# An encoder layer in one stream of matrix work: final blocks moved ahead of gate columns, output products by weight unit, last attention tiles split in place

## The chip, the cores and the metric

The kernel runs on one core of a Trainium2 chip. The metric is the device time in microseconds (us). One execution was profiled; its span is the time from its first to its last instruction. TensorE (PE) does the matrix products, PEld is its loading of weights, VectorE (DVE) and ScalarE (ACT) do elementwise work, GpSimd (POOL) little here, and SyncE (SP) issues nearly all DMAs.

## The reference

One layer of a bidirectional encoder, for two sequences: a short one of 1024 tokens (s = 0) and a long one of 2048 (s = 1), each with the same 16 meta tokens in front; the model width is 1024.

```python
xn = rmsnorm(h, g_pre)
proj = xn @ w_in + b_in                        # 1024 -> 6672 columns
na_q, na_k, na_v, na_z, ml_qk, ml_v, ml_z, ml_o, ml_g, mg = split(proj)
ya = (neighbourhood_attention(na_q, na_k, na_v, na_rpb) * silu(na_z)) @ w_a
yb = (mlstm_branch(ml_qk, ml_v, ml_g, ml_o, conv_w, head_g) * silu(ml_z)) @ w_b
ga, gb = split(sigmoid(mg))
y = (ga * ya + gb * yb) @ w_out
return h + rmsnorm(y, g_post)                  # meta tokens dropped
```

The attention looks at a window of 8 rows by 16 columns of a grid 64 wide, plus the meta tokens. The mLSTM runs forwards and backwards over the sequence; its queries and keys pass a convolution of three taps first. All is float32.

## The kernel before

**Precision.** Each operand of a dense product is split into a high part (a rounding to a shorter float32 form, made by ScalarE) and a low part (the rest, made by VectorE); each product is three matmuls: high x high, high x low, low x high (`mm3`, lines 170 to 172; `tm_unit`, lines 619 to 621; `prods`, lines 1875 to 1877). Weights are handled in units of 512 KB. At first use a unit is loaded raw (`wraw`), split (`whi`, `wlo`, lines 258 to 270) and both parts are written to DRAM; later uses load the two parts. Four units are held at a time (`NBW`), and `wtake`, `wdone`, `wpump` hand them out, give them back and fetch the next.

**Two streams.** `dense` yields the dense products in the order of `PLAN`, each step with its cost in us (0.235 for a matmul of 512 columns, 0.12 for 256). `sparse` yields the steps of the branches in the order of `STEPS`: mLSTM 0, attention 0, mLSTM 1, attention 1, each step with a cost. `run` puts the two together: after each sparse step it takes dense work worth the step's cost times the entry's rate (the last number in `STEPS`; a few "fix" steps are taken at 1). TensorE executes in exactly this order. The other engines' order is made by a planner with a cost model, except for instructions given to `behind`, which keep the program's order. A sparse stage starts only when what it needs is in `done`; until then `run` takes dense work alone. `beside` is called at each dense step: it steps the convolutions (`pstep`, `cprep`) and the background generators (`bg`).

**Dense work.** An entry (s, t0, letters) of `PLAN` is a group over 1024 tokens: column tiles of 128 (`fm_half`; a and k, q, z, G, h stand for mLSTM queries and keys, attention keys, queries, gates z, and the merge gates) and token-major columns (t: values, output gates; `tm_unit`). `layout` orders the jobs of a group: some jobs of column tiles, then all of t, then the rest. "S" is a Strassen-like pass over the short sequence (`sstream`). An entry ("f", s, b) is a final block over 512 tokens (`final`): eight pairs of half merges (attention half, mLSTM half; 12 matmuls of 512 columns each) give the gated sum `mh`, `mlo`; then the output product, four quarters of 256 columns (cq) by four tiles of 128 tokens (tt), 24 matmuls of 256 columns each; then the norm with `g_post` and the residual (`final_out`). The last final block has no successor (`nxt` is None).

**What meets around the change.** The attention writes its gated output `yg` to DRAM (`YA`); `yload` loads it into `yl`, ScalarE copies the high part to `yh`, VectorE subtracts, and the merge that needs it waits for that. The output product of a token tile ends with a square on ScalarE (line 1905, with an accumulated sum) and a product with the gain on VectorE (line 1906), both from PSUM. PSUM has eight banks, three of them under the tag `pj`. The inputs of the next group are built by `build_half`: tokens are loaded, squared and summed (`rsum`), a diagonal of the factors is made (`rdiag`), spread over the partitions by a matmul (`rrows`, line 326), and the transposed tokens are scaled by it and split. Final block 0 of a sequence can start once its mLSTM is through and the attention of its rows is done.

Of the kernel before, what the change touches and what calls it, by code (L numbers as in the profile page):

```python
# [43 lines left out]
PLAN = ((0, 0, "akt"),) + FIRST + ((1, 0, "at"), (1, 1024, "akqzt"), (1, 0, "kqzGh"), (1, 1024, "Gh"), ("f", 0, 0), ("f", 0, 1), ("f", 1, 0), ("f", 1, 1), ("f", 1, 2), ("f", 1, 3))  # L44
STEPS = (("ml", 0, (), 0.78), ("na", 0, (0, 1), 1.05), ("ml", 1, (), 0.78), ("na", 1, (0, 1, 2, 3), 0.765))
# [80 lines left out]
class K:  # L126
# [3 lines left out]
    def __init__(self, tc, ins, outs):  # L130
        self.tc, self.nc = tc, tc.nc
        self.xs = []
        self.i, self.o = ins, outs
        self.wreq, self.wraw, self.wrdy, self.wout = deque(), deque(), deque(), 0
        self.wseen, self.wkept, self.xkept = set(), {}, {}
        self.rwait = {}
        self.xput, self.turn, self.last, self.turns = deque(), 0, None, False
        self.need, self.gpost = False, None
# [4 lines left out]
        self.hold, self.early = deque(), True  # L143

# [47 lines left out]
    def gain(self, name):  # L192

        g = self.wp.tile([P, D], F32, name="gain", bufs=1)
        self.nc.sync.dma_start(g, _bc(self.i[name], 0, D))
        return g
# [99 lines left out]
    def rsum(self, xs, res, first=None):  # L296
# [7 lines left out]
        for q, (xr, n) in todo:  # L304
            junk = wp.tile([P, D], mybir.dt.bfloat16, name="xsq", tag="thT", bufs=1)
            nc.scalar.activation(junk[:n], xr[:n], AF.Square, accum_out=ss[:n, q:q + 1])
            yield
# [105 lines left out]

    def build_half(self, s, t0, res):
# [370 lines left out]
    def sload(self, n, u):  # L785
# [5 lines left out]
        def get(i, j, pool, name, tag, bufs):  # L791
            x = pool.tile([P, 4 * WU], F32, name=name, tag=tag, bufs=bufs) if tag == "wraw" else pool.tile([P, 2 * 512], F32, name=name, tag=tag, bufs=bufs)
            x = x[:, :1024].rearrange("p (a c) -> p a c", a=2)
            for a in range(2):
                self.nc.sync.dma_start(x[:, a], self.i["wu"][u0 + j + 2 * a, :, 512 * i:512 * i + 512])
# [107 lines left out]
    def sstream(self, visits, nxt):  # L903
# [9 lines left out]
        for n, u in self.sorder(visits):  # L913
            s, t0, c, v = self.sdq[n]
            if u == 1:
                q = self.sq[n] = dict(done=set())
                for a in range(2):
                    q["C", a] = self.psum(("pj", "pj", "pj", "sc")[(2 * n + a) % 4], [P, 512])
                if n == 0 and len(visits) > 1 and visits[1][:2] not in self.XF:
# [48 lines left out]
    def layout(self, cols):  # L968
# [6 lines left out]
        a = max(1, min(sum(c[0] < C_GA for _, c in jobs), len(jobs) - 1))  # L975
# [21 lines left out]
    def spread(self, gen, chunks, until=None):  # L997

        steps = 22 if until is None else 12
# [246 lines left out]
    def na_out(self, np_, unit, s):  # L1246
# [15 lines left out]
        if hh and cb == 3:  # L1262
            nc.vector.tensor_tensor(yg, yg, zt, op=ALU.mult)
            nc.sync.dma_start(self.YA[s][rt][pr][:, :], yg)
# [121 lines left out]
    def cprep(self, s, h, is_k, a, b):  # L1386
# [5 lines left out]
        if s:  # L1392
            both = self.wp.tile([P, D], F32, name="cpl", tag="gain", bufs=1)[:, :804].rearrange("p (a c) -> p a c", a=2)
# [34 lines left out]
    def pstep(self):  # L1428

        while len(self.pact) < 2 - ((1, 0) in self.have) and self.pq:  # L1430
# [128 lines left out]
    def ml_outputs(self, mp, s, h, g, NB, sts, norms):  # L1559
# [23 lines left out]
        def split(b):  # L1583
            if b < NB:
                raw = raws.pop(b)
                if s and b % 3 == 2 and self.gpost is None:
# [87 lines left out]
        def finish(b):  # L1674
# [9 lines left out]
            if not a:  # L1684
                hbs[q] = mp.tile([P, 2 * CB, P], F32, name="hb", bufs=2)
# [47 lines left out]
    def ml_norm(self, mp, s, h, q, hb, tz):  # L1733
# [20 lines left out]
        for _ in range(10):  # L1754
# [8 lines left out]
    def yload(self, s, b):  # L1763
# [17 lines left out]
        late, half = [4, 5, 6, 7, 0, 1, 2, 3], None  # L1781
        while todo or late or half is not None:
# [19 lines left out]
    def final(self, s, b, nxt):  # L1802
# [21 lines left out]
        for ft, br in [(0, 1)] + [x for f in range(KT) for x in ((f + 1, 1), (f, 0)) if x[0] < KT]:  # L1824
# [3 lines left out]
            for k in range(4 * br, 4 * br + 4):  # L1828
                self.need = True
                while k not in self.yk:  # L1830
                    if next(self.ygen) == "wait" and k not in self.yk:
# [25 lines left out]
        if self.fresh:  # L1857
            self.fresh = False
            nc.vector.tensor_scalar(self.gpost, self.gpost, -0.125, None, op0=ALU.mult)
# [10 lines left out]
        def prods(p, tt, ws, k0, k1):  # L1870
            o = p[:, :256]
            xs = slice(tt * P, tt * P + P)
            for k in range(k0, k1):
                wh, wl = ws[k // 4][0][:, k % 4, :], ws[k // 4][1][:, k % 4, :]
                nc.tensor.matmul(o, mh[:, k, xs], wh, start=k == 0, stop=False)  # L1875
                nc.tensor.matmul(o, mh[:, k, xs], wl, start=False, stop=False)  # L1876
                nc.tensor.matmul(o, ml[:, k, xs], wh, start=False, stop=k == KT - 1)  # L1877

        for cqs in (((0,), (1,), (2,), (3,)) if nxt else ((0,), (1,), (2, 3))):
            wq = [self.wtake(2) for _ in cqs]  # L1880
            first = {}
            if cqs[0] == 0:
                for tt in range(2):
                    first[tt] = self.psum("pj", [P, 512])
                    prods(first[tt], tt, wq[0], 0, 7)
                    yield 21 * C256
            turns = [(tt, x) for tt in range(4) for x in zip(cqs, wq)]
            if len(cqs) > 1:
                turns[1:3] = turns[2], turns[1]
            for tt, (cq, ws) in turns:  # L1890
                if tt in first:
                    p = first[tt]
                    prods(p, tt, ws, 7, 8)
                else:
                    p = self.psum("pj", [P, 512])
                    prods(p, tt, ws, 0, 4)
                    if tt == 3:
                        self.wdone()
                    yield 12 * C256
                    prods(p, tt, ws, 4, 8)  # L1900
                if tt == 3:
                    self.wdone()
                o = p[:, :256]
                dst = yt[tt][:, cq * 256:(cq + 1) * 256]
                nc.scalar.activation(sqj, o, AF.Square, accum_out=ssq[:, tt, cq:cq + 1])
                nc.vector.tensor_tensor(dst, o, self.gpost[:, cq * 256:(cq + 1) * 256], op=ALU.mult)
                if cq == 3 and not nxt:
                    for _ in self.final_out(s, t0, yt, ssq, tt, tt + 1):
                        pass
                if nxt and hook is None:  # L1910
                    if nxt[0] != "f":
                        nres = []
                        hook = self.build_half(*nxt[:2], nres)
                    else:
                        hook = self.ystart(*nxt[1:])
                if hook:
                    next(hook, None)
                yield (3 if tt in first else 12) * C256
# [10 lines left out]
    def final_out(self, s, t0, yt, ssq, a, b):  # L1929
# [17 lines left out]
        r = self.rsqrt8(fp, sv[:, a:b], [P, b - a])  # L1947
        yield
# [14 lines left out]
    def dense(self, ctx):  # L1963
# [11 lines left out]
        for j, item in enumerate(PLAN):  # L1975
# [6 lines left out]
            if s == "f":  # L1982
                if self.gpost is None:
                    self.gpost = self.gain("g_post")
                    self.fresh = True
# [111 lines left out]
```

## Time and profile before

| | us |
|---|---|
| median of 3 runs | 2817.07 |
| lowest, highest | 2802.38, 2821.04 |
| the profiled execution | 2810.6 |
| its span | 2808.8 |
| PE busy in the span | 2728.9 |
| DVE busy | 1729.2 |
| ACT busy | 1501.9 |

The profile's page gives busy times per engine; its other views group instructions by line and tiles, list who waited for whom, follow the chain of work that ended last, and cut the span into stages. Ends of matmuls are modelled, as they are pipelined: a busy PE need not be at its peak. A matmul of 512 columns is recorded with some 0.38 us while the next starts 0.23 us after it.

### The profile page before, as it was taken

What the parts mean: (1) busy time and instruction counts of PE and PEld (TensorE: products, weight loads), DVE (VectorE), ACT (ScalarE), POOL (GpSimd) and SP (SyncE); (2) the same over time, 40 slices, a digit from 0 to 9 for tenths busy, and PEclk for the clock granted to TensorE, in tenths of its full rate; (3) what the DMA queues carried; (4) which work ended last, traced back from release to release, by engine and by line L of the source; (5) the groups of instructions that cost most, each with busy time, mean ns of one, the idle gap of its engine ahead of it and who ended that gap; (6) DMA issues with size and microseconds to landing.
All of it is one profiled execution on the core that took longest, in us unless ns stands there. A gap on an engine that the chain in (4) does not pass through costs nothing.

```text
span 2808.8 us, 47866 instructions
## 1 busy us (share of the span) xinstructions
PE 2728.9 (97%) x16840; PEld 2427.4 (86%) x16840; DVE 1729.2 (62%) x4339; ACT 1501.9 (53%) x3348; POOL 124.4 (4%) x298
## 2 busy tenths in 40 slices
PE   8999999999999999999999999999999999999988
PEld 7899988879998778999977888888888898988978
DVE  5534664534667636566624767665667868787754
ACT  5222454433446646655534666565657676777731
POOL 0220000005000000320000000000000000000000
PEclk9999999999999999999999999999999999999989
DMA  9876753396656976756586566885599989898964
GB/s 370 327 252 216 241 181 105 104 349 203 189 171 200 328 232 203 224 178 212 189 286 208 196 208 203 275 280 172 171 314 327 292 268 302 247 323 281 275 216 174
DMA packets 354676, 666.47 MB, mean 237 GB/s; under 512 B 53796, under 2 KB 159220, under 8 KB 354436
## 3 DMA queue, kind: packets, MB, share of 16 engines
q1 hardware_dynamic: 347172, 654.37, 70.4%
q0 software_dynamic: 7264, 9.04, 1.2%
q8 instruction: 133, 2.18, 0.3%
q14 instruction: 107, 0.88, 0.1%
HBM read 446.24 MB, written 216.97 MB: 236 GB/s over the span
## 4 chain that ended last, share of the span: by engine, by line
PE 75%; DMA 14%; DVE 6%; ACT 3%; issue 1%; SPq 1%; DVEq 0%; ACTq 0%; POOLq 0%; POOL 0%
PE pj L170 11%; PE pj L171 11%; PE pj L172 11%; PE pj L619 6%; PE pj L621 6%; PE pj L620 6%; PE pj L1876 3%; PE pj L1875 3%; PE pj L1877 3%; PE sm L1254 2%; PE sm L172 2%; PE tr L1240 2%; PE sm L171 2%; PE sm L170 2%; DMA qk<-cpl 1%; DMA wlo<-wl 1%
## 5 line engine op out<-in xcount | busy, mean ns | idle before, releaser
L170 PE MATMUL pj<-xh,whi 128*128 128x512 f32 (+1 forms) x1480 | 581.7, 393 | 9.8 <-ACT st L544 7.8
L171 PE MATMUL pj<-xl,whi 128*128 128x512 f32 (+1 forms) x1480 | 567.9, 384 | 0.1
L172 PE MATMUL pj<-xh,wlo 128*128 128x512 f32 (+1 forms) x1480 | 566.6, 383 | 0.3 <-DVE wlo L270 0.3
L619 PE MATMUL pj<-whi,xh 128*128 128x256 f32 (+1 forms) x1536 | 438.8, 286 | 2.1 <-DVE stT L634 2.1
L620 PE MATMUL pj<-wlo,xh 128*128 128x256 f32 (+1 forms) x1536 | 432.5, 282 | 0.0
L621 PE MATMUL pj<-whi,xl 128*128 128x256 f32 (+1 forms) x1536 | 432.4, 282 | 0.0
L170 PEld LDWEIGHTS pj<-xh,whi 128*128 128x128 f32 x1480 | 280.2, 189 | 60.5 <-ACT st L544 8.6
L172 PEld LDWEIGHTS pj<-xh,wlo 128*128 128x128 f32 x1480 | 279.8, 189 | 58.0 <-DVE wlo L270 0.5
L171 PEld LDWEIGHTS pj<-xl,whi 128*128 128x128 f32 x1480 | 280.4, 189 | 46.5 <-issue 0.5
L619 PEld LDWEIGHTS pj<-whi,xh 128*128 128x128 f32 x1536 | 289.6, 189 | 2.7 <-DVE stT L634 2.3
L620 PEld LDWEIGHTS pj<-wlo,xh 128*128 128x128 f32 x1536 | 289.4, 188 | 0.2
L621 PEld LDWEIGHTS pj<-whi,xl 128*128 128x128 f32 x1536 | 289.3, 188 | 0.0
L1875 PE MATMUL pj<-whi,mh 128*128 128x256 f32 x768 | 222.1, 289 | 6.5 <-ACT whi L269 3.7
L1876 PE MATMUL pj<-wlo,mh 128*128 128x256 f32 x768 | 218.9, 285 | 3.8 <-DMA wlo<-wl 2.1
L1877 PE MATMUL pj<-whi,mlo 128*128 128x256 f32 x768 | 218.4, 284 | 0.0
L170 PE MATMUL pj<-yh,whi 128*128 128x512 f32 x384 | 156.6, 408 | 9.7 <-ACT yh L1793 9.7
L1875 PEld LDWEIGHTS pj<-whi,mh 128*128 128x128 f32 x768 | 147.5, 192 | 8.3 <-ACT whi L269 4.1
L171 PE MATMUL pj<-yl,whi 128*128 128x512 f32 x384 | 153.2, 399 | 1.3 <-DVE yl L1778 1.3
L172 PE MATMUL pj<-yh,wlo 128*128 128x512 f32 x384 | 152.7, 398 | 0.0
L1876 PEld LDWEIGHTS pj<-wlo,mh 128*128 128x128 f32 x768 | 147.5, 192 | 5.7 <-DMA wlo<-wl 2.6
L1877 PEld LDWEIGHTS pj<-whi,mlo 128*128 128x128 f32 x768 | 147.4, 192 | 0.0
L1243 DVE TENSOR_TENSOR pts<-tr,pts 96x384 fp32r<-96x384 f32 (+2 forms) x192 | 118.6, 618 | 46.7 <-ACT pts L1242 45.8
(378 smaller groups left out, 5643.8 us busy)
## 6 DMA issues: line engine op xcount, KB each, us to landing
whi<-wh SPq DMA_DIRECT2D x152, 512.0 KB
wlo<-wl SPq DMA_DIRECT2D x152, 512.0 KB
wraw<-wu SPq DMA_DIRECT2D x64, 512.0 KB
wh<-whi SPq DMA_DIRECT2D x64, 512.0 KB
wl<-wlo SPq DMA_DIRECT2D x64, 512.0 KB
gt<-st SPq DMA_DIRECT2D x96, 256.0 KB
tg<-gt SPq DMA_DIRECT2D x96, 256.0 KB
xt<-xt SPq DMA_DIRECT2D x32, 512.0 KB
```

The lines of the kernel that those rows point to most:

```text
L170: mm(out, ah, bh, start=start, stop=False, **more)
L171: mm(out, ah, bl, start=False, stop=False, **more)
L172: mm(out, al, bh, start=False, stop=stop, **more)
L619: nc.tensor.matmul(o, xh, wh, start=k == 0, stop=False)
L620: nc.tensor.matmul(o, xh, wl, start=False, stop=False)
L621: nc.tensor.matmul(o, xl, wh, start=False, stop=k == KT - 1)
L1240: nc.tensor.transpose(pt[:ks, ch, :], pr_[:, ch * ks:(ch + 1) * ks], self.ident)
L1243: nc.vector.tensor_tensor(pts[:ks, :nb, 1, :], pt[:ks, :nb], pts[:ks, :nb, 0, :].bitcast(F32), op=ALU.subtract)
L1254: nc.tensor.matmul(av[:, cb % 2], vt[:ks, kc // 8 + ch].rearrange("p a b -> p (a b)"), pts[:ks, ch].rearrange("p a b -> p (a b)"), start=c ...
L1875: nc.tensor.matmul(o, mh[:, k, xs], wh, start=k == 0, stop=False)
L1876: nc.tensor.matmul(o, mh[:, k, xs], wl, start=False, stop=False)
L1877: nc.tensor.matmul(o, ml[:, k, xs], wh, start=False, stop=k == KT - 1)
```

## The change

1. `PLAN`: the final blocks of the short sequence stand ahead of the last group of gate columns of the long one. The rates of `STEPS` for mLSTM 1 and attention 1 become 0.81.
2. `final`: the output product goes by weight unit (half of the contraction, 512 rows, of one quarter): one unit is used for all four token tiles, whose accumulators lie two to a bank in two banks, then the second unit. In the last block this holds for two quarters; the other two go by tile as before, in another order, with four units held. In the last block two half merges change places.
3. `na_out`: when the final block that is being loaded is the one whose attention tile has just ended, `yg` is split straight into `yh`, `yl`, without DRAM.
4. `rahead`: the factors of the long sequence's first two halves are made during the Strassen pass and kept.
5. The convolutions of the long sequence use other buffers (four under the tag `xr`, which token loads use too, in place of one), two are active at a time, and `beside` steps them twice.
6. `layout`: t comes after at most two jobs of column tiles. That changes the group (1, 1024, "akqzt") alone.
7. `g_post` is loaded by quarters for each final block, and its factor of -0.125 is applied in `final_out`. `hb` has three buffers, a norm waits 12 steps in place of 10, and `build_half` is stepped faster by `spread`.

```diff
-PLAN = (... (1, 0, "kqzGh"), (1, 1024, "Gh"), ("f", 0, 0), ("f", 0, 1), ("f", 1, 0), ("f", 1, 1), ("f", 1, 2), ("f", 1, 3))
-STEPS = (("ml", 0, (), 0.78), ("na", 0, (0, 1), 1.05), ("ml", 1, (), 0.78), ("na", 1, (0, 1, 2, 3), 0.765))
+PLAN = (... (1, 0, "kqzGh"), ("f", 0, 0), ("f", 0, 1), (1, 1024, "Gh"), ("f", 1, 0), ("f", 1, 1), ("f", 1, 2), ("f", 1, 3))
+STEPS = (("ml", 0, (), 0.78), ("na", 0, (0, 1), 1.05), ("ml", 1, (), 0.81), ("na", 1, (0, 1, 2, 3), 0.81))
...
+    def gain(self, c):
+        g = self.wp.tile([P, WU], F32, name="gp", tag="bb", bufs=2)
+        self.nc.sync.dma_start(g[:, :256], _bc(self.i["g_post"], 256 * c, 256))
+        return g[:, :256]
...
+    def rahead(self, s, t0s):
+        dg = self.wp.tile([P, 2, 512], F32, name="dgs", tag="gain", bufs=1)
+        for c, t0 in enumerate(t0s):
+            toks, r = self.tokens(s, t0, range(4), self.wp, 4), []
+            for _ in range(3):
+                yield
+            yield from self.rsum(toks, r, pin=True)
+            self.rpre[s, t0] = self.rdiag(r[0], dg[:, c])
+            yield
...
         else:
-            toks, r = self.tokens(s, t0, range(4), wp, 4), []
-            yield
-            yield from self.rsum(toks, r)
-            dg = self.rdiag(r[0], toks[3][0])
+            dg = self.rpre.pop((s, t0), None)
+            if dg is None:
+                ...
...
         self.pstep()
+        if (1, 0) in self.have:
+            self.pstep()
...
-        a = max(1, min(sum(c[0] < C_GA for _, c in jobs), len(jobs) - 1))
+        a = max(1, min(2, len(jobs) - 1))
...
-            nc.sync.dma_start(self.YA[s][rt][pr][:, :], yg)
+            if self.y and self.y[0] == (s, rt) and pr in self.ylate:
+                _, yh, yl = self.y
+                nc.scalar.activation(yh[:, pr], yg, AF.Copy)
+                nc.vector.tensor_tensor(yl[:, pr], yg, yh[:, pr].bitcast(F32), op=ALU.subtract)
+                self.ylate.remove(pr)
+                self.yk.add(pr)
+            else:
+                nc.sync.dma_start(self.YA[s][rt][pr][:, :], yg)
...
-            both = self.wp.tile([P, D], F32, name="cpl", tag="gain", bufs=1)...
+            both = self.wp.tile([P, D], F32, name="cpl", tag="xr", bufs=4)...
...
-        while len(self.pact) < 2 - ((1, 0) in self.have) and self.pq:
+        while len(self.pact) < 2 and self.pq:
...
+        order = [(0, 1)] + [x for f in range(KT) for x in ((f + 1, 1), (f, 0)) if x[0] < KT]
+        if not nxt:
+            order[2:4] = order[3], order[2]
...
+        def prods(o, tt, w, a, fresh):
+            xs = slice(tt * P, tt * P + P)
+            for k in range(4):
+                f, q = 4 * a + k, w[0][:, k, :]
+                nc.tensor.matmul(o, mh[:, f, xs], q, start=fresh and f == 0, stop=False, skip_group_check=True)
+                nc.tensor.matmul(o, mh[:, f, xs], w[1][:, k, :], start=False, stop=False, skip_group_check=True)
+                nc.tensor.matmul(o, ml[:, f, xs], q, start=False, stop=f == KT - 1, skip_group_check=True)
+
+        def leave(o, tt, cq, gp):
+            nc.scalar.activation(sqj, o, AF.Square, accum_out=ssq[:, tt, cq:cq + 1])
+            nc.vector.tensor_tensor(yt[tt][:, cq * 256:(cq + 1) * 256], o, gp, op=ALU.mult)
+
+        gps = [self.gain(0), self.gain(1)]
+        for cq in range(4 if nxt else 2):
+            banks = [self.psum("pj", [P, 2, 256]) for _ in range(2)]
+            for a in range(2):
+                w = self.wtake(1)[0]
+                for tt in range(4):
+                    o = banks[tt // 2][:, tt % 2]
+                    prods(o, tt, w, a, tt % 2 == 0)
+                    if tt == 3:
+                        self.wdone()
+                    if a:
+                        leave(o, tt, cq, gps[cq])
+                        ...
+                    yield 12 * C256
+            if cq < 2:
+                gps.append(self.gain(cq + 2))
+        if not nxt:
+            ws = [[self.wtake(1)[0] for _ in range(2)] for _ in range(2)]
+            turns = [(0, 2), (1, 2)] + [x for tt in range(2, 4) for x in ((tt - 2, 3), (tt, 2))] + [(2, 3), (3, 3)]
+            ...
```

More of the change, by code (lines that the diff above doesn't have):

```diff
@@ L1830, in final @@
                 while k not in self.yk:
[L1831 removed]
+                    if next(self.ygen, "wait") == "wait" and k not in self.yk:
                         yield True
@@ new lines, in final @@
+                    if hook:
+                        next(hook, None)
+                    yield 12 * C256
+            if cq < 2:
[3 more added lines that the diff above has]
+            turns = [(0, 2), (1, 2)] + [x for tt in range(2, 4) for x in ((tt - 2, 3), (tt, 2))] + [(2, 3), (3, 3)]
+            for tt, cq in turns:
+                o = self.psum("pj", [P, 512])[:, :256]
+                for a in range(2):
+                    prods(o, tt, ws[cq - 2][a], a, True)
+                    if a == 0:
+                        yield 12 * C256
+                leave(o, tt, cq, gps[cq])
+                if cq == 3:
@@ L1908, in final @@
                     for _ in self.final_out(s, t0, yt, ssq, tt, tt + 1):
                         pass
[L1910 to L1918, printed above, removed]
+                yield 12 * C256
```

86 lines of the change are left out of this document (32 added, 54 removed).

## The prediction

> **What bounds the kernel now.** First the page's busy times, then TensorE's groups (busy, mean ns, and after the second bar the idle time in front of them), then a table of stages.
>
> ```profile
> span 2808.8 us, 47866 instructions
> ...
> PE 2728.9 (97%) x16840; PEld 2427.4 (86%) x16840; DVE 1729.2 (62%) x4339; ACT 1501.9 (53%) x3348; POOL 124.4 (4%) x298
> ```
>
> TensorE works or waits in its pipeline for 97% of the span, and the change leaves the number and the shapes of its dense matmuls alone. So only its 80 us without a matmul, and the stretches at a low clock, can be won; nothing that shortens another engine's work counts by itself, and a new gap in TensorE's queue counts in full.
>
> ```profile
> L1875 PE MATMUL pj<-whi,mh 128*128 128x256 f32 x768 | 222.1, 289 | 6.5 <-ACT whi L269 3.7 <-DMA whi<-wh 2.8
> L1876 PE MATMUL pj<-wlo,mh 128*128 128x256 f32 x768 | 218.9, 285 | 3.8 <-DMA wlo<-wl 2.1 <-DVE wlo L270 1.7
> ...
> L170 PE MATMUL pj<-yh,whi 128*128 128x512 f32 x384 | 156.6, 408 | 9.7 <-ACT yh L1793 9.7
> ```
>
> Output products wait 6.5 + 3.8 = 10.3 us for weights; one merge waits 9.7 us, once. The stages (length, then busy time of PE, PEld, DVE, ACT, POOL, then granted clock, DMA share, GB/s):
>
> ```profile
> 562.00:592.00 30.00, 25.95 (x99) 19.85 (x98) 17.72 (x32) 17.55 (x27) 0.59 (x13) 0.89 1.03 374
> 1775.00:2043.00 268.00, 267.88 (x1409) 226.00 (x1408) 164.85 (x552) 156.63 (x422) 1.30 (x3) 1.00 0.67 223
> 2060.00:2182.00 122.00, 115.77 (x736) 105.86 (x736) 87.28 (x177) 81.20 (x175) 0.00 (x0) 0.96 0.94 317
> 2182.00:2690.00 508.00, 495.33 (x3279) 451.08 (x3278) 403.36 (x945) 360.18 (x809) 2.06 (x4) 0.99 0.89 279
> 2690.00:2714.00 24.00, 12.30 (x59) 9.90 (x56) 13.78 (x34) 4.17 (x10) 0.00 (x0) 0.79 0.79 277
> 2714.00:2809.00 95.00, 85.98 (x543) 77.73 (x543) 40.66 (x107) 12.99 (x41) 0.00 (x0) 0.93 0.53 189
> ```
>
> The reader sees full stages (1775 to 2043: mLSTM beside gate columns, 0.1 us lost) and leaky ones: the first final block (6.2 us idle at clock 0.96), the next four (12.7 us in 508), and the end of the last attention (11.7 of 24 us, clock 0.79).
>
> **The change, part by part**
>
> *Last outputs split in place.* The chain of waits at the end of the attention:
>
> ```profile
> 2705.29 0.70 DVE yg L1263
> 2706.01 4.43 DMA ya<-yg
> 2710.45 3.24 DMA yl<-ya
> 2714.40 0.80 PE pj L170
> ```
>
> The two DMAs, 2706.0 to 2713.7, go; the copy to the high part and TensorE's start, 0.7 us, stay. So the merge could start near 2706.7. The reordered last block also puts one more half merge (12 matmuls of 0.235 us, 2.8 us) ahead of the product that needs this tile, so the 9.7 us vanish. After the gap TensorE runs slowly: the clock of 0.93 over 95 us, part of which is the idle tail; I take 3 us. **-13 us** (-9 to -15). Late next is the attention itself, whose idle in 2690 to 2701 stays. The residual and output DMAs stand on SP's queue as before; two fewer for each tile done in place.
>
> *Long factors early.*
>
> ```profile
> 569.46 7.01 DMA xr<-x_sample
> ...
> 581.42 2.08 PE tr L326 x2
> ```
>
> The factor of the second half of the long sequence is computed at the end of the Strassen stream, with tokens loaded then; TensorE has 4.05 us idle in 562 to 592 and a clock of 0.89 (3 us more). With the factors made a column pass earlier, beside matmuls that fill that stage, **-6 us** (-3 to -7).
>
> *Values sooner, convolutions in pairs, rates.* One row each from four answers, count, durations, first and last start: attention 0's products, the gates of mLSTM 1, attention 1's products, the convolutions' first step.
>
> ```profile
> L1254 PE MATMUL sm<-pts,vt x224: 278/282/384, 1036.3 to 1398.1; 96*128 96x256 f32 x56, 104*128 104x256 f32 x56
> L1306 PE MATMUL sm<-g_lf,tri x4: 221/274/275, 1463.6 to 1463.9; 128*128 128x68 f32 x4
> L1254 PE MATMUL sm<-pts,vt x448: 274/282/582, 2101.4 to 2701.1; 128*128 128x256 f32 x74, 96*128 96x256 f32 x38, 104*128 104x256 f32 x38
> L1407 ACT ACTIVATE cpl<-cpl,cw x48: 402/617/632, 927.5 to 1512.4; 128x384 f32<-128x384 f32 x36, 128x128 f32<-128x128 f32 x8, 128x400 f32<-128x400 f32 x4
> ```
>
> The gap of 65 us from 1398 to 1463 is mLSTM 1 waiting for the convolutions: about 24 us of it the plan's fixed lead, about 40 us their drain. Two at a time and stepped twice a turn, the 48 of 7 steps take 168 turns of 1.44 us dense work, some 270 us from 927, so they end near 1200 and the drain goes. TensorE loses nothing by it today (dense work fills the gap), so nothing is won directly: 40 us of dense work are pushed later. The new rates take them up: by the plan's costs mLSTM 1 is 579 units, 579 x 0.03 = 17 us more dense work, attention 1 is 576, 576 x 0.045 = 26 us more. 43 against 40: the last block meets the attention's end where it does now. The convolutions' buffers now share the four that build the next inputs near 930; I put **-1 us** (-8 to +10) on the whole.
>
> *Short merges ahead of the last gate columns.* By the same costs, at attention 0's end dense work still has some 30 us of columns and 28 column tiles of 48 matmuls (316 us at 0.235) before the first final block; mLSTM 1 takes 579 x 0.81 and 34 fixed, 503 us. So the first final block (192 x 0.235 + 384 x 0.12 = 91 us) and 0.7 of the second move beside the mLSTM, and the 180 us of gate columns beside attention 1. What VectorE does for the final blocks, of 2060 to 2690:
>
> ```profile
> L1841 DVE SCALAR_TENSOR_TENSOR tg<-tg,pj 128x512 f32<-128x512 f32 x80 | 54.3, 680 | 12.7 <-PE pj L172 7.2 <-issue 3.5 <-DMA tg<-gt 1.1
> ...
> L1906 DVE TENSOR_TENSOR yo<-pj,gain 128x256 f32<-128x256 f32 x79 | 33.1, 420 | 19.4 <-ACT sqj L1905 18.6
> L1845 DVE TENSOR_TENSOR mlo<-tg,mh 128x512 fp32r<-128x512 f32 x40 | 27.4, 686 | 3.3 <-ACT mh L1844 2.8
> L1843 DVE TENSOR_TENSOR tg<-tg 128x512 f32<-128x512 f32 x40 | 27.4, 685 | 0.4
> L1778 DVE TENSOR_TENSOR yl<-yl,yh 128x512 fp32r<-128x512 f32 x40 | 27.1, 680 | 0.0
> ...
> L270 DVE TENSOR_TENSOR wlo<-wraw,whi 128x1024 fp32r<-128x1024 f32 x14 | 17.1, 1222 | 7.2 <-ACT whi L269 7.2
> ```
>
> A block costs VectorE 169.3 / 5 = 34 us, the first 20 more (16 weights x 1.22). The mLSTM holds it for 164.85 / 268 = 0.615 of the time. The moved stretch is 157 us of dense work, about 196 us with the mLSTM's matmuls: 121 + 54 + 24 = 199 us by these rows, some 10% less where recorded instructions overlap. VectorE is as long as TensorE there. Cost **+7 us** beyond the next item (0 to +30).
>
> *Output products by unit.* A weight unit is used for four token tiles before the next is needed, and units are released one by one: of the 10.3 us of waits and about 5 us at the low clock in 2060 to 2182 I take **-12 us** (-5 to -15). But four accumulators now share two banks, and tiles 0 and 1 (2 and 3) follow each other in one bank while the first is being read out. How long a read-out takes, in the last block:
>
> ```profile
> 2762.75 0.28 PE L1877 MATMUL pj<-whi,mlo 128*128 128x256 f32 x1
> ...
> 2763.13 0.38 ACT L1905 ACTIVATE sqj<-pj 128x256 bf16<-128x256 f32 x1 [2.29 <-PE pj L1877]
> ...
> 2763.64 0.42 DVE L1906 TENSOR_TENSOR yo<-pj,gain 128x256 f32<-128x256 f32 x1 [2.34 <-ACT sqj L1905]
> ```
>
> Two things are seen. VectorE's product waits for ScalarE's square although it takes nothing from it: they share the bank. And the bank is free at 2764.06, where the next matmul could have started at 2762.87 (0.12 after the last): 1.19 us. That columns don't matter shows in the mLSTM's states:
>
> ```profile
> L1555 DVE SCALAR_TENSOR_TENSOR st<-st,g_fb,sm 128x130 f32<-128x130 f32 x88 | 30.7, 348 | 51.4 <-ACT st L1553 46.9 <-PE sm L172 1.8
> ```
>
> L1555 reads columns 130 to 259 of a bank whose columns 0 to 129 L1553 reads, and still waits for it. So I expect TensorE to wait at the second of each pair. These are 2 waits x 4 passes x 5 blocks + 2 x 2 in the last = 44. Behind the waiting matmul stands all of TensorE's queue, the sparse branch's matmuls too. From 1.19 us goes what attention puts between two chunks: four blocks of 91 us in 508 less 12.7 idle leave 131 us of attention, 0.36 for each us of dense work, 0.5 us for a chunk of 1.44. To it comes the queue in front of the two readers (VectorE busy 79% there, half of a 0.69 us operation, 0.3 us). 0.95 x 40 + 1.19 x 4 = **+43 us** (+32 with engines free at once, +52 without cover; 0 if TensorE doesn't wait).
>
> The Trainium skill, PSUM — Partial Sum Buffer, section "PSUM bank collisions raise a hardware error", asks for guarding by bank and quadrant, reads against reads and disjoint columns included. The two waits above agree; by guarding of bytes alone the sum would be 43 us less.
>
> *Gains by quarter.* Four loads of 128 KB a block come onto SP's queue in place of one in all; the third and fourth may wait there for the last read of their buffer, about 1.2 us, with weight loads behind them. Three weight units of 5.8 us each lie ahead of TensorE and hide that: 0, and 6 x 2 x 1.2 = 14 us without that cover.
>
> *The tail.* One more small operation (about 0.15 us) on the last chain, and the last two tiles finish a turn closer: **+1 us** (0 to +2).
>
> **Sum**: -13 - 6 - 1 + 7 - 12 + 43 + 1 = +19. The profiled run took 2810.6 us, its span 2808.8; so 2830 us. The median shown, 2817.07, lies 6.5 us higher and the three runs are 18.7 us apart, so one per cent (28 us) is about what can be told.
>
> **Rivals**
> - *TensorE doesn't wait* (dependencies go by columns): -43, and VectorE's stretch costs 15 in place of 7: 2830 - 35 = 2795 (2775 to 2810). For it: no row shows a matmul held by a read of other columns. Against it: the two waits quoted.
> - *VectorE becomes the bound beside the mLSTM.* If it reaches only its share of 2182 to 2690, 0.79, the 179 to 199 us take 227 to 252 us in place of the 222 I count (196 + 19 of the waits + 7): 2830 + 20 = 2850 in the middle. For it: ordered queues with two chains. Against: slices with 0.88 that lost little.
> - *Slower: dense work runs out.* The rates take 43 us more; if the drain isn't saved, the last block is reached up to 40 us early and attention runs alone, with TensorE idle half the time as in 2690 to 2714, and each us missing is added at the end: 2830 + 40 = 2870. It decides from the point where mLSTM 1's gates come later than about 1430.
> - *Clock.* If the 1 us gaps lower the clock to the 0.79 of 2690 to 2714 over the six half passes (about 29 us each), that adds 174 x 0.27 = 46: 2876. Against it: 0.96 in 2060 to 2182 with such gaps. The Trainium skill, TensorE: Matmul & The Clock Gate, "A second HAM failure mode: psum-queue depth-cycling", describes that.
>
> **How the numbers follow.** Forecast 0.48 (own range 2812 to 2848), no wait 0.25, VectorE 0.13, dense work out 0.08, clock 0.03, others 0.03. Faster by over 1% (below 2789) needs the lower part of "no wait" and luck: 0.17. Slower (above 2845): most of VectorE, the two below it and the forecast's edge: 0.28. Same 0.55. The range leaves a tenth at each end: 2780 to 2862.
>
> **What would show it.** Right: TensorE waiting for the product with the gain (now L1906) some 40 times, about 1 us each, in pairs within the output passes; no DMA between the last yg and the last merge; no wait of L326 near 580; gates of mLSTM 1 near 1430; VectorE above 0.85 in the first final block. Wrong: no such waits of TensorE, or attention running alone for tens of us at the end.

## The result, and the profile after

| | before | after |
|---|---|---|
| median of the runs compared, us | 2815.65 (2802.38 to 2821.04) | 2848.62 (2845.46 to 2854.67) |
| ratio, with its 95% interval | | 1.0131 [1.0096, 1.0166] |
| the profiled execution, us | 2810.6 | 2854.67 |
| its span, us | 2808.8 | 2852.7 |

The changed kernel is slower: 33 us by the medians, 44 by the profiled executions. The forecast was 2830, that is +19 on the profiled execution; the median lies inside the range and just above 2812 to 2848, the forecast's own. The sign of the sum was right, its size was not.

The page of the changed kernel, its busy times and the three groups that answer to those shown of before (busy, mean ns, then idle time in front):

```profile
span 2852.7 us, 47899 instructions
...
PE 2742.3 (96%) x16840; PEld 2431.9 (85%) x16840; DVE 1727.5 (61%) x4347; ACT 1502.6 (53%) x3348; POOL 124.8 (4%) x298
...
L1905 PE MATMUL pj<-whi,mh 128*128 128x256 f32 x768 | 226.5, 295 | 47.2 <-DVE yo L1911 46.8
...
L171 PE MATMUL pj<-yh,whi 128*128 128x512 f32 x384 | 158.1, 412 | 0.0
...
L1906 PE MATMUL pj<-wlo,mh 128*128 128x256 f32 x768 | 219.1, 285 | 0.0
```

The work is the same (16840 matmuls, TensorE busy 13 us longer). What is new stands behind the second bar: the output product's first matmul waits 46.8 us for VectorE's product with the gain. The waits for weights (6.5 + 3.8 us) are gone from these groups, and the merge no longer waits for `yh` (9.7 us before, 0.0 now). The table of who waited for whom, TensorE's part (total us, times, longest):

```profile
PE pj L1905 <- DVE yo L1911: 46.8, 40, 4.6
PE pj L329 <- ACT xr L321: 8.3, 2, 4.5
...
PE pj L171 <- DMA whi<-wh: 5.4, 2, 2.9
```

Forty times, as announced, and nothing else is near it. The same table over the first two final blocks (1826 to 2109):

```profile
PE pj L1905 <- DVE yo L1911: 23.4, 14, 4.6
```

and beside the attention (2340 to 2736):

```profile
PE pj L1905 <- DVE yo L1911: 19.1, 22, 2.4
```

Eight of the 14 waits belong to the first block's output product (1897 to 1971, beside the mLSTM) and cost 1.67 us each. Six belong to the second's (2044 to 2109): five of about 1.07 us behind the mLSTM's end, and one of 4.65 at its end. Beside the attention a wait costs 0.87 us. The two longest, 4.21 us at 1952 and 4.65 at 2072, are not the work of a full VectorE alone. Before the first, the square stood behind work of ScalarE that had waited for the load of `qk` and then for VectorE; before the second, VectorE itself was idle for the load of `szg`, and the product with the gain stood behind that in its queue:

```profile
1948.37 0.63 ACT L1621 ACTIVATE qkw<-qk 128x512 fp32r<-128x512 f32 x1 [3.15 <-DMA qk<-qk]
...
2071.02 0.69 DVE L1783 TENSOR_TENSOR hb<-hb,szg 128x512 f32<-128x512 f32 x1 [5.79 <-DMA szg<-sz]
2071.63 0.41 DVE L1911 TENSOR_TENSOR yo<-pj,gp 128x256 f32<-128x256 f32 x1
2072.10 0.58 PE L1905 MATMUL pj<-whi,mh 128*128 128x256 f32 x1 [4.65 <-DVE yo L1911]
```

In the last block, where nothing stands beside, the timeline shows one whole:

```profile
2803.17 0.28 PE L1907 MATMUL pj<-whi,mlo 128*128 128x256 f32 x1
2803.55 0.38 ACT L1910 ACTIVATE sqj<-pj 128x256 bf16<-128x256 f32 x1 [1.00 <-PE pj L1907]
...
2804.05 0.42 DVE L1911 TENSOR_TENSOR yo<-pj,gp 128x256 f32<-128x256 f32 x1 [1.05 <-ACT sqj L1910]
...
2804.53 0.39 PE L1905 MATMUL pj<-whi,mh 128*128 128x256 f32 x1 [1.08 <-DVE yo L1911]
...
2804.76 0.28 PE L1906 MATMUL pj<-wlo,mh 128*128 128x256 f32 x1
```

The reader sees the chain that the prediction drew: last matmul, square, product, and only then the next token tile in the other half of the same bank. The bracket says 1.08 us, but the loss is larger. Matmuls of this form follow each other at 0.12 us; here 1.36 us pass from start to start (1.24 lost), and the one after starts 0.23 us later in place of 0.12. So a listed wait of 1.08 costs 1.35 us, 0.27 more than the list says. Over 40 waits that makes 46.8 + 40 x 0.27 = 57.6 us, an estimate from this one instance. Counted in the same way, from start to start, for each of the 40 waits, the trace gives 58 us: 15.5 in the first block, 11.9 in the second, 25.4 beside the attention and 5.3 in the last block.

The table of stages (length, busy PE, PEld, DVE, ACT, POOL, granted clock, DMA share, GB/s):

```profile
562.00:592.00 30.00, 29.92 (x127) 23.19 (x125) 15.54 (x19) 10.71 (x15) 0.71 (x13) 1.00 1.04 375
1826.00:2044.00 218.00, 192.45 (x1141) 170.66 (x1140) 178.37 (x519) 127.36 (x341) 0.00 (x0) 0.95 0.82 287
2109.00:2340.00 231.00, 230.96 (x1182) 193.43 (x1181) 125.66 (x309) 153.56 (x315) 1.02 (x2) 1.00 0.68 212
2340.00:2736.00 396.00, 370.11 (x2424) 333.25 (x2424) 289.55 (x665) 264.75 (x587) 1.04 (x2) 1.00 0.79 256
2792.00:2852.00 60.00, 46.93 (x385) 45.91 (x383) 22.38 (x84) 8.24 (x33) 0.00 (x0) 0.95 0.40 144
```

The full stage (gate columns) and the leaky ones (final blocks) have changed places, as planned. Gate columns beside the attention lose nothing. The final blocks beside the mLSTM lose 25.6 of 218 us, with VectorE at 0.82. The stretch near 580 lost 4.05 us before and is full now.

### The profile page after: what moved, and what is told of

Same layout as the page of the kernel before. It is cut to its first block, busy times and chain, and to the rows that moved or that the text cites. A ratio compares the mean times of both kernels' runs of the same rounds, so it can differ in the third digit from the quotient of the medians.

```text
span 2852.7 us, 47899 instructions
## 1 busy us (share of the span) xinstructions
PE 2742.3 (96%) x16840; PEld 2431.9 (85%) x16840; DVE 1727.5 (61%) x4347; ACT 1502.6 (53%) x3348; POOL 124.8 (4%) x298
## 4 chain that ended last, share of the span: by engine, by line
PE 81%; DMA 9%; DVE 5%; ACT 3%; issue 1%; SPq 1%; POOL 0%; DVEq 0%; ACTq 0%
PE pj L171 13%; PE pj L172 13%; PE pj L173 13%; PE pj L638 6%; PE pj L639 6%; PE pj L640 6%; PE pj L1905 3%; PE sm L1277 2%; PE pj L1907 2%; PE pj L1906 2%; PE tr L1263 2%; PE sm L173 2%; PE sm L172 2%; PE sm L171 2%; DMA nv<-stT 1%
## 5 line engine op out<-in xcount | busy, mean ns | idle before, releaser
L171 PE MATMUL pj<-xh,whi 128*128 128x512 f32 (+1 forms) x1480 | 583.4, 394 | 9.4 <-DMA whi<-wh 5.4
L171 PEld LDWEIGHTS pj<-xh,whi 128*128 128x128 f32 x1480 | 280.8, 190 | 59.1 <-issue 7.3
L1905 PE MATMUL pj<-whi,mh 128*128 128x256 f32 x768 | 226.5, 295 | 47.2 <-DVE yo L1911 46.8
L171 PE MATMUL pj<-yh,whi 128*128 128x512 f32 x384 | 158.1, 412 | 0.0
```

The costliest lines, as they stand in the source:

```text
L171: mm(out, ah, bh, start=start, stop=False, **more)
L1905: nc.tensor.matmul(o, mh[:, f, xs], q, start=fresh and f == 0, stop=False, skip_group_check=True)
```

## The experiments

The experiments ran in three sets, each set on one chip together with the kernel before; each ratio is to the kernel before of its own set, and its interval is 4 to 7 us to either side (10 us for the changed kernel). The kernel before took 2812.84 us in the first set (alternating, by tile, gates first, unpinned), 2816.23 in the second (units alone, by tile with gates first, through DRAM, no early factors) and 2811.31 in the third (units alternating, the convolutions, the best version). Two experiments of one set are compared by medians, two of different sets by their ratios, times 2815. The difference of two experiments is uncertain by 6 to 11 us.

**Neighbouring tiles in different banks.** The theory of the bank says that the waits go if tiles 0 and 1 no longer share a bank; the rival is that VectorE or the clock is the limit whatever the bank.

```diff
-                    o = banks[tt // 2][:, tt % 2]
-                    prods(o, tt, w, a, tt % 2 == 0)
+                    o = banks[tt % 2][:, tt // 2]
+                    prods(o, tt, w, a, tt < 2)
```

> Of the changed kernel, the two token tiles that share a bank no longer follow each other: tiles 0 and 2 share one bank, 1 and 3 the other, and a chunk of 1.44 us of another bank stands between them. Theory (TensorE waits for the read-out of the bank it writes to): the 46.8 us of waits for the product with the gain fall to under 10, and the time from 2848.6 to 2790-2805 us. Rival (the time is lost because VectorE is too busy beside the mLSTM, and the bank is only where it shows): TensorE waits elsewhere, at least 30 us of the waits come back under other lines, and the time stays above 2830 us.

Measured: 2791.86 us, ratio 0.9923 [0.9905, 0.9942]. These two lines make 56.8 us (2848.62 - 2791.86; 59 by the ratios, with 11 to either side) and turn a slower kernel into a faster one. TensorE's part of the waits, its longest entries and the one for the product with the gain:

```profile
PE tr L1788 <- DVE hb L1783: 9.5, 4, 3.2
PE pj L171 <- DMA whi<-wh: 5.4, 2, 4.2
...
PE pj L1905 <- DVE yo L1911: 0.9, 3, 0.5
```

The wait for the product with the gain has fallen from 46.8 us to 0.9, and nothing of its size took its place. The 58 us counted above from start to start agree with the time that came back, within its interval. All later experiments on the changed kernel build on this one, except those by tile, where each tile has a bank of its own.

**Output products by tile, in the changed kernel.** The changed kernel with the product loops of before, each tile with a bank of its own.

```diff
-        for cq in range(4 if nxt else 2):
-            banks = ...
-            ...
+        for cqs in (((0,), (1,), (2,), (3,)) if nxt else ((0,), (1,))):
+            wq = [self.wtake(2) for _ in cqs]
             ...
+            turns = [(tt, x) for tt in range(4) for x in zip(cqs, wq)]
```

> The changed kernel with the output products of the first two to four quarters by token tile again, as before the change, each accumulator in a bank of its own and a quarter's two weight units at once; all else as changed. Bank theory: the 46.8 us go, the waits for weights (10.3 us before) come back: 2800-2815 us. Rival (the move of the final blocks beside the mLSTM costs the time): 2835-2850 us.

Measured: 2783.43, 0.9899 [0.9883, 0.9916], lower than expected. The waits for weights that the order by unit was to remove do not come back when it goes: no output product waits for a weight in its list. In this order of work the product by unit earns nothing, and is some 8 us worse, which is no more than the two intervals allow by chance.

**Units alone, in the kernel before.** The kernel before with nothing but the product by unit, once with the shared neighbours of the change, once alternating.

```diff
...
+        for cq in range(4 if nxt else 2):
+            banks = [self.psum("pj", [P, 2, 256]) for _ in range(2)]
+            for a in range(2):
+                w = self.wtake(1)[0]
+                for tt in range(4):
+                    o = banks[tt // 2][:, tt % 2]        # second kernel: banks[tt % 2][:, tt // 2]
+                    prods(o, tt, w, a, tt % 2 == 0)      # second kernel: tt < 2
+                    ...
```

> The kernel before with one part of the change: output products by weight unit, tiles 0 and 1 (2 and 3) in one bank, the last two quarters of the last block by tile in the order of before. Bank theory: 44 waits of TensorE for the product with the gain, about 1 us each where attention runs beside, so 40 to 55 us slower than before (2853 to 2868 us against 2812.8). Rival (the waits cost much only beside the mLSTM, where VectorE and ScalarE are full): under 30 us slower.

> The kernel before with output products by weight unit alone (as in e9), but with neighbouring token tiles in different banks. If the shared bank is all that made e9 slow, the 37 us go; if units also save the waits for weights, as forecast with 12 us, the ratio to before is 0.995 to 0.997. If they save none, it is 0.999 to 1.001.

Measured: shared 2853.27, 1.0134 [1.0106, 1.0162]; alternating 2801.11, 0.9968 [0.995, 0.9985]. The list of the first:

```profile
PE pj L1874 <- DVE yo L1880: 39.0, 42, 2.2
```

This one edit makes the kernel before as slow as the whole change did. 42 waits, 0.93 us each. The two ratios are 1.66% apart, 47 us, all of it the place of the accumulators; the list plus 0.27 us for each wait gives 50. The order by unit without the shared bank saves 9 us (0.32% of 2811) here, where the weights did wait.

**Gate columns first again.** The alternating kernel with the order of `PLAN` of before.

```diff
-PLAN = (... (1, 0, "kqzGh"), ("f", 0, 0), ("f", 0, 1), (1, 1024, "Gh"), ("f", 1, 0), ...)
+PLAN = (... (1, 0, "kqzGh"), (1, 1024, "Gh"), ("f", 0, 0), ("f", 0, 1), ("f", 1, 0), ...)
```

> Alternating banks (e1), but the last gate columns stand ahead of the short sequence's final blocks, as before the change. If VectorE beside the mLSTM is the bound of the moved blocks, this is 10 to 20 us faster than e1. If only the shared banks cost time there, it is within 5 us of e1. If the move saves waits for weights in the first final block (10.3 us before), it is 8 to 15 us slower than e1.

Measured: 2777.95, 0.9874 [0.9857, 0.9891], 13.9 us below the alternating kernel. Its stages, gate columns beside the mLSTM, then final blocks beside the attention:

```profile
1826.00:2046.00 220.00, 220.00 (x1139) 185.25 (x1138) 129.54 (x436) 126.11 (x323) 2.38 (x8) 1.00 0.65 208
2046.00:2290.00 244.00, 237.73 (x1570) 216.09 (x1570) 190.62 (x425) 172.71 (x384) 1.02 (x2) 0.99 0.97 317
```

and in the alternating kernel the final blocks beside the mLSTM:

```profile
1826.00:2073.00 247.00, 231.46 (x1534) 211.28 (x1533) 193.63 (x583) 141.01 (x385) 2.38 (x8) 0.98 0.92 313
```

Beside the mLSTM the final blocks lose 15.5 us of TensorE, beside the attention 6.3. The clocks (0.98 of 247 us against 0.99 of 244) make some 2.5 us more, an estimate; the rest of the 14 us is not placed. The gate columns lose nothing beside either branch. So moving the short merges costs 14 us and wins nothing that these stages show. Half of what the blocks lose beside the mLSTM stands in one row of the waits, of the alternating kernel from 1826 to 2073:

```profile
PE tr L1788 <- DVE hb L1783: 7.8, 3, 3.2
```

That is the mLSTM's own transpose waiting for a product on VectorE; in the same stretch one of these products stood 4.4 us for the load of `szg`. So VectorE's queue is the place, but how much of it is VectorE's load and how much such waits for loads, no run separates.

**By tile and gates first together.**

```diff
 both edits above
```

> The changed kernel with output products by token tile (e2) and the last gate columns ahead of the short sequence's final blocks. If the two edits are independent, e2's gain over e1 (8 us) and e6's (14 us) add up: about 2770 us. Rival (by tile, the first final block beside attention waits for weights as it did before, 10 us): 2778 to 2785 us.

Measured: 2776.54, 0.9872 [0.9846, 0.9897]. Against the alternating kernel the two edits gave 8 and 14 us singly, and by the ratios 14 together. So they may win in part the same loss, but the interval of the 14 is about 9 us to either side, and 22 is not excluded.

**Attention's last outputs through DRAM again.**

```diff
-            if self.y and self.y[0] == (s, rt) and pr in self.ylate:
+            if False:
```

> Alternating banks (e1), but the attention's last outputs go through DRAM again. Theory: the two DMAs (7.7 us), less what the half merge put ahead covers, and the slow clock after the gap come back: 6 to 13 us above e1's 2791.9. Rival (other dense work now covers the end): within 3 us of e1.

Measured: 2802.01, 0.9952 [0.9936, 0.9969]; by the ratios (it ran in another set) 8 us above the alternating kernel. In its list of waits the merge waits for the high part again:

```profile
PE pj L171 <- ACT yh L1824: 3.8, 1, 3.8
```

The split in place is worth about 8 us. The wait without it is 3.8 us and not 9.7; the half merge that was put ahead should cover 2.8 us of that (12 matmuls of 0.235 us), and the rest is not explained.

**No early factors.**

```diff
-                if n == 1:
-                    self.bg.append(self.rahead(nxt[0], (nxt[1], nxt[1] + 512)))
```

> Alternating banks (e1), but the factors of the long sequence's first two halves are made where they were before, in the last part of the Strassen pass, with their squares in program order. If the early factors bring what was forecast, 3 to 7 us above e1. Rival (the start of the next group waits for weights behind the written-back inputs on the DMA queues, so nothing is won): within 3 us of e1.

Measured: 2800.2, 0.9953 [0.9937, 0.9968], 8 us above the alternating kernel by the ratios. The stage in which the factors were late, without the early factors:

```profile
492.00:632.00 140.00, 133.47 (x564) 105.04 (x563) 66.06 (x123) 62.55 (x95) 0.91 (x15) 0.98 0.66 236
```

and with them, in the alternating kernel:

```profile
492.00:632.00 140.00, 133.32 (x560) 104.36 (x559) 59.19 (x93) 52.98 (x78) 0.71 (x13) 0.98 0.58 206
```

TensorE is busy for the same time in both. The wait near 580 goes, and the next group then waits for its weights (the 5.4 us of L171 for `whi` in the first list), which come behind the group's inputs: the chain of waits of the changed kernel has the DMAs `xh<-xh`, `xl<-xl` and `wlo<-wl` one after the other there. In the profiled executions the same number of matmuls has started 1.0 us later at 1809 and 9.0 us later at 2058: the 8 us appear beside the mLSTM; why is not settled.

**Squares of the early factors not pinned.**

```diff
-            if pin:
-                self.behind(sq)
```

> Alternating banks (e1), and the squares of the factors are no longer kept in program order on ScalarE. Theory: the 8.3 us that TensorE waits for the factors of the long sequence's second half (two waits near 894 and 954) come from squares held back behind other ScalarE work, so the time is 5 to 14 us below e1. Rival: the waits come from the buffers that convolutions and token loads now share; then the time is within 3 us of e1 and the two waits stay.

Measured: 2787.49, 0.9913 [0.9895, 0.9931], 4 us below the alternating kernel, with intervals that overlap. The two waits of L329, 4.5 us for ScalarE and 3.8 for VectorE in the alternating kernel, shrink to one of 1.1. The gates of mLSTM 1 come at 1421.5 in place of 1428.4, but the mLSTM's last outputs at 2031.5 in place of 2029.9: what was won by then is lost again, and where was not traced.

**Convolutions one at a time, and the rates.** First kernel: one convolution active, one step a turn, rates of before. Second: the same with the changed rates.

```diff
-STEPS = (... ("ml", 1, (), 0.81), ("na", 1, (0, 1, 2, 3), 0.81))
+STEPS = (... ("ml", 1, (), 0.78), ("na", 1, (0, 1, 2, 3), 0.765))   # first kernel only
-        if (1, 0) in self.have:
-            self.pstep()
-        while len(self.pact) < 2 and self.pq:
+        while len(self.pact) < 2 - ((1, 0) in self.have) and self.pq:
```

> Alternating banks (e1), but one convolution of the long sequence at a time, stepped once a turn, and the two rates of before (0.78 and 0.765). By the forecast's accounting (the drain of 40 us of dense work and the higher rates cancel, nothing is won directly): within 8 us of e1 (ratio 0.989 to 0.995). Rival (convolutions out of the way help the start of mLSTM 1, whose waits were 10 us before): 8 to 15 us above e1.

> As e10, but with the changed kernel's rates (0.81 twice). By the forecast's rival on dense work running out, the last block is reached up to 40 us early and attention ends alone: 20 to 40 us above e10. If the rates matter little, within 8 us of e10.

Measured: first 2782.41, 0.9888 [0.9863, 0.9912]; second 2809.99, 0.9997 [0.9982, 1.0012]. The gates of mLSTM 1 (last start) in the first:

```profile
L1334 PE MATMUL sm<-g_lf,tri x8: 195/274/279, 621.0 to 1467.2; 128*128 128x36 f32 x4, 128*128 128x68 f32 x4
```

and in the second, with the attention's last outputs:

```profile
L1334 PE MATMUL sm<-g_lf,tri x8: 195/274/279, 623.2 to 1465.3; 128*128 128x36 f32 x4, 128*128 128x68 f32 x4
...
L1284 DVE TENSOR_TENSOR yg<-yg,zt x24: 671/686/693, 1083.4 to 2716.9; 128x512 f32<-128x512 f32 x24
```

Both have the drain of the convolutions (gates at 1467 and 1465). With the higher rates and the drain, dense work runs short and the time rises by 28 us (31 by the ratios). In two stretches of the second kernel no matmul of the dense stream starts; the next one is a merge of attention outputs, and the attention runs alone:

```profile
2554.30:2573.80 19.50, 11.13 (x63) 9.11 (x62) 18.36 (x48) 15.35 (x33) 0.51 (x1) 0.82 0.84 289
2700.80:2715.20 14.40, 10.05 (x49) 8.18 (x48) 11.57 (x28) 7.32 (x17) 0.00 (x0) 0.75 0.84 289
```

TensorE is idle for 12.7 of these 33.9 us, at a lower clock; the longest such stretch beside the attention's last 250 us in the first kernel is 4.5 us. This is the mechanism of the rival "dense work runs out", below the 40 us that I gave it. The first is 10 us faster than the alternating kernel by the ratios (9 to either side): pairs and rates together cost, where I had put about nothing. But with the changed rates the pairs win 21 us (0.9997 against 0.9923). Pairs with the old rates, the fourth of the four, were not run.

**The best version.** By tile, gate columns first, squares not pinned; all else as in the change.

> The changed kernel with output products by token tile, the last gate columns ahead of the short sequence's final blocks, and squares free in order: the edits that e2, e6 and e5 point to. If e5's 3 us add to e8: ratio 0.984 to 0.987 (2771 to 2778 us); if the order of squares only moves waits about: 0.987 to 0.990.

Measured: 2771.8, 0.9855 [0.9834, 0.9877], the lowest median of all, though its interval overlaps that of by tile and gates first; 40 us under the kernel before and 77 under the changed one. Its page:

```profile
span 2768.9 us, 47923 instructions
...
PE 2718.1 (98%) x16840; PEld 2419.0 (87%) x16840; DVE 1726.1 (62%) x4347; ACT 1497.1 (54%) x3348; POOL 124.8 (5%) x298
```

## Why the prediction was right, and where its sizes were off

The terms, in us, with what the runs gave (undoing one part in the alternating kernel, except for the units):

| term | forecast | measured | from |
|---|---|---|---|
| TensorE waits for the read-out of a shared bank | +43 | +57, or +59 by the ratios (+47 in the kernel before) | alternating; units alone |
| VectorE beside the mLSTM (short merges moved) | +7 | +14 | gates first |
| units save waits for weights | -12 | -9 in the kernel before; +8 in the changed one | units alternating; by tile |
| in-place split | -13 | -8 | through DRAM |
| early factors | -6 | 0 in its stage, -8 over the whole | no early factors |
| convolutions in pairs, rates | -1 | +10 | convolutions one at a time |

**The sign comes from the bank alone.** The other terms of the forecast add up to -24, and the alternating kernel, without the shared bank, lies 21 us under the kernel before. That agreement is luck: the single terms were off by 2 to 20 us, in both directions, as the table shows.

**The bank: right in mechanism and count, too small in price.** 44 waits were counted, 40 and 42 are listed. The step that failed is "0.95 x 40 + 1.19 x 4". It took 0.5 us off each wait for attention chunks in between, in all blocks but the last. The first block's product stands beside the mLSTM, and its waits cost 1.67 us listed, 1.94 from start to start; the first two blocks together cost 27 us where the sum has 15. Two waits of over 4 us behind loads, which it did not foresee, are 9.7 of these 27. Beside the attention the waits cost 1.15 from start to start and not 0.95. The last block, at 1.35 for the instance above, was priced 1.19. The upper end that I gave for no cover, +52, was nearer. The wait holds for disjoint columns, as the edit of two lines shows, and the rival "TensorE doesn't wait" fell with it. By the Trainium skill, PSUM — Partial Sum Buffer, section "PSUM bank collisions raise a hardware error", accesses to disjoint columns of a bank must be kept apart too; the waits of the trace agree, and no run here tried the access without them.

**VectorE: right in direction, half the size.** The stretch holds 178.37 us of VectorE in 218, the 0.82 near which the rival "VectorE becomes the bound" was worked out. That rival named 2850, which is nearly the time measured, but not for its reason alone: 57 us of the difference go with the bank while VectorE's work stays. The sign named, VectorE above 0.85 in the first final block, shows in its merges alone: 62.86 of 65 us from 1832 to 1897, but 46.15 of 74 in its output product, from 1897 to 1971. In part the other engines act by making read-outs late: the eight waits of 1.67 in place of 0.87 are 6 us of the bank's term, 3 of them the one long wait at 1952.

**Dense work: the balance of 43 against 40 held, the price did not.** Gates at 1434 (forecast about 1430), as this row of the changed kernel shows, and the convolutions ended at 1243 (forecast 1200):

```profile
L1336 PE MATMUL sm<-g_lf,tri x4: 221/274/275, 1434.0 to 1434.3; 128*128 128x68 f32 x4
```

The last block met the attention as before (the longest stretch at the attention's end without a dense matmul is 7.5 us, 10.1 before), and the rival of 2870 did not happen. Still pairs and rates together cost 10 us against one convolution with the old rates. Why is open: buffers shared near 930 and the rates were not separated.

**In place and early factors.** The first was over-priced by 5 us, which is within the interval of 7: in the new order of half merges the wait it removes is 3.8 us and no longer 9.7. For the second, the step "beside matmuls that fill that stage" failed: something else was late next, the weights.

**Clock.** By stage the granted clock is 0.95 in two stages with the waits and 1.00 in the third, which has 22 of them; the rival took 0.79. Cut finer, the changed kernel shows where it falls:

```profile
1900.00:1951.00 51.00, 40.79 (x329) 39.20 (x327) 36.20 (x99) 31.70 (x94) 0.00 (x0) 1.00 0.89 307
1952.00:1960.00 8.00, 7.50 (x42) 7.50 (x43) 2.06 (x5) 1.76 (x6) 0.00 (x0) 0.61 0.43 146
...
2072.00:2080.00 8.00, 6.82 (x35) 6.53 (x36) 0.89 (x3) 0.95 (x4) 0.00 (x0) 0.65 0.30 122
...
2792.00:2846.00 54.00, 46.93 (x385) 45.91 (x383) 19.14 (x72) 8.24 (x33) 0.00 (x0) 1.00 0.39 140
2846.00:2852.00 6.00, 0.00 (x0) 0.00 (x0) 3.24 (x13) 0.00 (x0) 0.00 (x0) 0.50 0.47 176
```

Five waits of 0.96 to 1.95 us between 1900 and 1951 leave it at 1.00, as do the four in the last block, where it falls only behind the last matmul. It falls behind the two waits of 4.21 and 4.65 us, and that costs at most 6 us (8 x 0.39 + 8 x 0.35). So the rival's mechanism, that gaps of 1 us lower the clock, did not happen; only the two gaps of over 4 us have a lower clock behind them. The other low spells of 1826 to 2044 (1826 to 1900 at 0.96, 2005 to 2044 at 0.87) have none of the waits in them. The Trainium skill, TensorE: Matmul & The Clock Gate, section "A second HAM failure mode: psum-queue depth-cycling", tells of a kernel whose short gaps between groups of matmuls sent the clock down and up again; the 38 shorter waits of this trace do not show that.

**What stays open.** The measured terms don't add up. Taking away the bank leaves 2791.86, 21 us under the kernel before, while the other measured parts sum to about -1 (14 - 9 - 8 - 8 + 10). Some 20 us of gain, or 37 with the +8 that the units showed in the alternating kernel itself, must belong to parts that no run undid singly (values sooner, gains by quarter, three buffers of `hb`, the faster `spread`, the order of the last block), or to parts that act on each other. One part can be placed: from the start of the attention's last product with the values to the end of the span the profiled executions take 107.7 us before, 100.8 in the run through DRAM and 93.4 in the alternating kernel. So some 7 us beside the split in place lie in the last block, whose order changed; no run undid that order alone.

## What to carry to other kernels

When two accumulators share a PSUM bank, let consecutive chunks alternate between banks, so that one bank's readers run while TensorE fills the other: two index expressions were worth 57 us of 2849. Before moving work beside another branch, compare the engine it loads, not only TensorE: the final blocks load VectorE more than the gate columns (0.78 against 0.59 of the time beside the mLSTM), and only the latter stood there without loss. In an engine's ordered queue look also for a load that the work in front waits for: two such waits made 9.7 of the 58 us. And price a gap of TensorE by starts of matmuls, since the listed idle time leaves out what the pipeline still has to do.

## What the runs showed of the hardware that I had not expected

A listed wait of 1.08 us cost 1.35 us, as the recorded 0.28 us of a matmul is longer than the 0.12 us between two, and the second matmul after a wait follows at 0.23. The granted clock stayed at 1.00 behind waits of 0.16 to 2.40 us and fell, to 0.61 and 0.65 of the next 8 us, behind the two of 4.21 and 4.65; what lies between was not met.
